# A hybrid decoder layer on one core: one softplus for both decays, bias tables read from memory, a minimum as the exponential's bias, and the planner's priorities set anew

## The chip, the cores and the metric

The program runs on one core of a Trainium2 chip. The metric is the time of one execution on the device in microseconds (us). The core has a matrix engine (TensorE, PE in the profile; PEld is its weight load), a vector engine (VectorE, DVE), a scalar engine (ScalarE, ACT), GpSimd (POOL) and a queue for DMAs (SyncE, SP). Each works through its own list of instructions in order and waits at semaphores for the others.

## The reference

One post-norm layer over 256 tokens of width 1024. A projection of the input gives the columns of four groups of six heads (head width 64); each group's output is multiplied by its own SiLU gate; the four are joined, projected back, added to the input and normalized.

```
proj = x @ w_in                              # 256 x 1024 by 1024 x 5906
a: softmax(q k / 8 - slope * dist) v         # causal; one block at this length
b: xbc = silu(conv4(xbc)); dt = softplus(dt_raw + dt_bias)
   y = ssd(xs * dt, -exp(A_log) * dt, B, C) + D * xs;  rms_norm(y * silu(z))
c: the three dilations of one head share a softmax: softmax(q k / 8 - slope * dist + ln count) v
d: q, k, v = silu(conv4(qkv)); q, k normalized; beta = sigmoid(b)
   g = -exp(A_log) * softplus(a + dt_bias);  gated delta rule in chunks, rms_norm, gate
out = layer_norm(2 ** 0.25 * x + concat(a, b, c, d) @ w_out)
```

In c a key that several dilations reach counts several times, so the mixture is one softmax whose scores carry the logarithm of the count.

## The kernel before

Weights arrive in blocks of up to 512 KB in a ring of four buffers (`raw`, line 403). Each block is split in two parts of lower precision: ACT copies the high part (`whi`), DVE subtracts it from the block (`wlo`), in `split` (line 418). PE multiplies high by high, high by low and low by high, three passes for each product, either with 128 weight columns as the stationary operand against all 256 tokens (`channels`, line 495) or with tokens as the stationary operand against 384 to 396 columns (`tokens`, line 517). These products, the stream, make up most of PE's work. The blocks come in the order: keys of d, gate d, queries of d (conv q), gate s, values c, values of d (conv v), conv bc, conv x, scores c, scores a, values a, and then the output weights.

Between these, small work is fed in. The delta path is: `softplus` of the decay (line 549), which is a chain of 16 DVE instructions and one ACT exponential on 12 numbers per partition; `decays` (line 566), which makes the decay matrix E; the products M and A (line 720); a triangular solve of 32 x 32 blocks on DVE, 31 steps over the tile Ub that read BL (line 785); a join on PE (line 798); and the delta rule itself (line 813). The state-space group has a softplus and a `decays` of its own (lines 750 to 755). Attention c and a (line 626) work on pairs of heads: PE makes scores, DVE adds the bias table, reduces to the row's maximum in the same instruction and writes p, a small DVE instruction multiplies the maximum by -0.125, ACT takes the exponential with that as its bias, divides, PE transposes and multiplies with the values. The bias table of c is computed by six DVE instructions (line 934), that of a by six ACT instructions (line 941) from constants `csb` that come in two loads early in the program (lines 448 and 450). The table of a (`biasa`) lies in the place s4, which BL has before it; that of c (`biasc`) lies in s3, which a block of the first weights has before it.

The order on each engine is not the program's. Every call is recorded with a modelled cost and its dependencies (`_Engine`, `Plan.add`), and `Plan.run` (line 200) then writes all orders out at build time. In each step it takes, over all engines, the instruction that can start first; among those of one engine that can start at about the same time (`AHEAD`) it takes the one with the longest way to the end plus the bias of its part in `PRIO`. Kinds of PSUM banks have limits (`LIMIT`) and are handed out in program order within a kind; a modelled cost is halved where two small matmuls lie side by side in the array. The engines then follow that order whatever the real times are.

Of the kernel before, what the change touches and what calls it, by code (L numbers as in the profile page):

```python
# [12 lines left out]
AF = mybir.ActivationFunctionType  # L13
# [13 lines left out]
LATE = ("moba", "dil", "lnc")  # L27


def _shape_constants():  # L30
    t = np.arange(128)
    row, col = t[:, None], t[None, :]
    parts = {
        "ident": row == col,
        "tri": row <= col,
        "suf": row > col,
    }
    dist = 128 + row - np.arange(256)[None, :]
    parts["moba"] = np.where(dist >= 0, -dist, -1e30)
    count = ((dist >= 0) & (dist <= 128)).astype(int) + ((dist >= 0) & (dist % 4 == 0)) \  # L40
        + ((dist >= 0) & (dist % 16 == 0))
    parts["dil"] = np.where(count > 0, -dist, -1e30)
    parts["lnc"] = 8.0 * np.log(np.maximum(count, 1))
    h = np.arange(6)[None, :]
    parts["sel"] = (row == h) | (row == 32 + h)
    at, n = {}, 0
    for k, v in sorted(parts.items(), key=lambda kv: kv[0] in LATE):
# [8 lines left out]
NEAR = CAT["moba"][0]  # L56
# [4 lines left out]
SWITCH, PORT, AHEAD = 0.17, 0.9, {"dve": 0.015, "pe": 0.185}  # L61
# [5 lines left out]
PRIO = {"split": -6.8, "conv k": 1086.3, "gate d": -51.1, "decay d": 1000.2, "norm k": 1627.6, "conv q": 1480.8,  # L67
        "products": 1504.1, "norm q": 1768.9, "gate s": 323.3, "decay s": -1394.4, "values c": 263.3,
        "conv v": 246.6, "blocks": 124.5, "join": -297.8, "delta": 975.5, "conv bc": -546.4, "conv x": -369.3,
        "state": 595.2, "scan": 1273.9, "scores c": -1234.3, "attention c": 2093.1, "scores a": -183.7,  # L70
        "values a": -1630.5, "attention a": -481.0, "out": 94.7, "out 0": -1157.7, "out 1": -1399.5,
        "ln 0": -2309.4, "ln 1": 877.3}
# [5 lines left out]
LIMIT = {"pj": 5, "g": 6, "ed": 1, "es": 5, "n": 6, "m": 4, "d": 4, "o": 1, "td": 5, "b": 2, "s": 2, "ts": 4, "c": 6, "ct": 5, "cv": 6, "a": 4, "at": 1, "av": 1}  # L78
BEGIN, SLOW = 1.2, 2.5


class Plan:
# [11 lines left out]
    def __init__(self, found=None):  # L94
        self.ops, self.tiles, self.tags, self.masks = [], {}, {}, {}
        self.after, self.bias, self.stream = None, 0.0, False
        self.found, self.made, self.slots = found, 0, {}

# [53 lines left out]
    def add(self, eng, call, cost, outs, ins, dma=0.0, mode=None, port=False, place=None, slow=0.0):  # L152
        i = len(self.ops)
        if self.found:
            self.ops.append({"id": i, "call": call, "dma": dma})
            return
        deps = {} if self.after is None else {self.after: 0.0}
        op = {"id": i, "bias": self.bias, "stream": self.stream, "eng": eng, "call": call, "cost": cost, "dma": dma,
              "mode": mode, "port": port, "place": place, "slow": slow, "deps": deps, "succ": [], "homes": []}
        self.ops.append(op)  # L160

        def dep(j, raw):
            if j != i:
                deps[j] = max(deps.get(j, 0.0), self.lat(j, eng) if raw or self.ops[j]["eng"] != eng else 0.0)

        for ap, write in [(a, False) for a in ins] + [(a, True) for a in outs]:
            info = self.tiles.get(ap.tensor.name)
            if info is None:
                continue
            p0, p1, m = self.region(info, ap)  # L170
            hit = lambda e: e[1] < p1 and p0 < e[2] and e[3] & m
            for e in info["w"]:
                if hit(e):
                    dep(e[0], True)
            if write:
# [24 lines left out]
    def run(self):  # L200
# [48 lines left out]
        while len(order) < len(ops):  # L249
# [22 lines left out]
            cost = o["cost"] * (0.5 if o["mode"] and o["mode"] == mode and o["place"] != place else 1.0)  # L272
# [94 lines left out]
def hybrid_layer(ctx, tc, plan, xT, x, w_in, w_out, convw, small, ln_g, ln_b, cst, out):  # L367
# [9 lines left out]
    def part(name):  # L377
        plan.bias = PRIO.get(name, 0.0)

# [60 lines left out]
    def constants():  # L440
# [54 lines left out]
    def channels(c0, n):  # L495

        for j in range(n // 128):
            hi, lo = split(load(w_in, 0, KC, c0 + j * 128, 128))
# [18 lines left out]
    def tokens(c0, n, raw=(), kinds=("pj", "pj")):  # L517

        bs = [bank(t) for t in kinds]
        for k0 in range(0, KC, 2):  # L520
            hi, lo = split(raw[k0 // 2] if k0 // 2 < len(raw) else load(w_in, k0 * 128, 2, c0, n))
# [6 lines left out]
        for i in range(2):  # L528
            yield i, bs[i]
# [90 lines left out]
    def scores(m, cols, tag):  # L620
        qk[m] = new(m + "qk", 2, 3, S, tag=tag)
        for n in range(2):
            for j, b in channels(cols[n], W):
                act.activation(qk[m][:, n, j, :], b, AF.Copy)

    def attention(m, k0, bias, tag):
# [5 lines left out]
        for pr in range(3):  # L632

            ss, pts = [bank(m) for _ in halves], []
# [4 lines left out]
            for e, s_ in enumerate(ss):  # L639
                h = 2 * pr + e  # L640
                p, mx = new("p", W), new("mx", 2, 2)
# [16 lines left out]
                pts.append(pt)  # L658
            b = bank(m + "v")
# [21 lines left out]
    beta, dav, gdec = new("beta", 2, 6), new("dav", 2, 6), new("gdec", 2, 6)  # L681
# [34 lines left out]
    part("conv q")  # L716
    for j, b in channels(D_Q, 256):
        conv(7 + j, b, kq[:, j, :, 1, :])
# [3 lines left out]
    for i in range(2):  # L722
        for pr in range(3):
            gb = [bank("m"), bank("m")]
# [93 lines left out]
    for i in range(2):  # L818
# [6 lines left out]
        for r in range(2):  # L825
            tp = slice(64 * r, 64 * r + 64)
# [11 lines left out]
        if i == 0:  # L838
# [5 lines left out]
            for e in range(2):  # L844
                q = slice(64 * e, 64 * e + 64)
                dve.tensor_copy(St[q, :, e, :], b[q, :3 * HD].rearrange("p (k d) -> p k d", k=3))
        ob = bank("o")
# [61 lines left out]
    for i in range(2):  # L909
        y = yd[:, i, :]  # L910
        b = bank("s")
# [22 lines left out]
    for h in range(NH):  # L934
        dve.scalar_tensor_tensor(bc[:, h, :], C("dil"), float(8 * SLOPES[h]), C("lnc"), op0=OP.mult, op1=OP.add)
# [5 lines left out]
    for h in range(NH):  # L941
        act.activation(ba[:, h, :], C("moba"), AF.Copy, scale=float(8 * SLOPES[6 + h]))
# [19 lines left out]
    for kk in order:  # L962
        part("out")
        plan.after = gate_in
# [100 lines left out]
```

## Time and profile before

| | us |
|---|---|
| median of 3 runs | 235.43 (235.09 to 236.21) |
| the profiled execution, whole | 235.13 |
| its span, first to last instruction | 233.4 |
| TensorE busy | 221.6 |
| VectorE busy | 178.6 |
| ScalarE busy | 142.2 |
| GpSimd busy | 22.3 |

The busy times are of the one profiled execution. A matmul's end is modelled in the profile and matmuls overlap, so the starts of successive matmuls tell PE's pace, and its busy time tells only where it had nothing at all. Nearly all instructions have the line of one helper (L356), so tiles and not lines tell the work apart: `ps` is any PSUM bank, `raw`, `whi`, `wlo` are the weight blocks, `sp` is the softplus's scratch, `mx` the row's maximum and sum, `p` the probabilities.

### The profile page before, as it was taken

The numbers are of one execution on the slowest core, as the hardware profiler recorded it, in microseconds if no ns is written. First come the engines' busy times: TensorE is split into PE (matmuls) and PEld (weight loads), VectorE is DVE, ScalarE is ACT, GpSimd is POOL, SyncE is SP. The second block draws the span as 40 slices with busy tenths as digits, with TensorE's granted clock in tenths as the row PEclk, the third lists the DMA queues.
The fourth block names the chain that finished last, engine by engine and source line by source line (L and its number), as shares of the span: only waits on it lengthen the run. The fifth ranks groups of instructions, "written<-read, shape, count | busy, mean of one in ns | idle before, by whom it ended". The sixth has DMA issues, their size and how long they took to land.

```text
span 233.4 us, 4547 instructions
## 1 busy us (share of the span) xinstructions
PE 221.6 (95%) x1679; PEld 198.2 (85%) x1679; DVE 178.6 (77%) x448; ACT 142.2 (61%) x300; POOL 22.3 (10%) x26
## 2 busy tenths in 40 slices
PE   7999999999999999899999999899999999999970
PEld 3999999699998999899888889697889988877870
DVE  2876999898869998899999996542579865464275
ACT  4777684656782544944669387999955547352210
POOL 3023020300020000000000000000023320000071
PEclk9999999999999999999999999999999999999997
DMA  6999627987550198666923524750525507550013
GB/s 177 357 368 325 186 84 200 272 215 212 144 152 14 18 262 237 172 183 179 260 79 81 145 73 128 192 161 4 176 94 183 179 4 246 204 180 3 0 67 113
DMA packets 45957, 36.92 MB, mean 158 GB/s; under 512 B 5600, under 2 KB 42592, under 8 KB 45936
## 3 DMA queue, kind: packets, MB, share of 16 engines
q1 hardware_dynamic: 45504, 36.25, 53.6%
q10 hardware_dynamic: 432, 0.39, 0.5%
q8 instruction: 13, 0.21, 0.3%
q14 instruction: 8, 0.07, 0.1%
HBM read 35.00 MB, written 1.64 MB: 157 GB/s over the span
## 4 chain that ended last, share of the span: by engine, by line
PE 42%; DVE 30%; DMA 11%; ACT 9%; issue 4%; SPq 2%; DVEq 0%; ACTq 0%
PE ps L356 42%; DVE wlo L356 10%; DMA raw<-in_w_in_dram 10%; DVE Ub L356 5%; DVE cy L356 4%; ACT whi L356 2%; DMA lead<-in_w_in_dram 2%; SPq L356 2%; DVE p L356 1%; DVE M L356 1%; DVE A L356 1%; ACT p L356 1%; ACT Ed L356 1%; DVE r L356 1%; ACT Tb L356 1%
## 5 line engine op out<-in xcount | busy, mean ns | idle before, releaser
L356 ACT ACTIVATE whi<-raw 128x1024 fp32r<-128x1024 f32 (+3 forms) x57 | 56.9, 1001 | 37.5 <-PE ps L356 25.6
L356 DVE TENSOR_TENSOR wlo<-raw,whi 128x1024 fp32r<-128x1024 f32 (+3 forms) x56 | 64.1, 1153 | 18.1 <-ACT whi L356 15.5
L356 PE MATMUL ps<-xhi,whi 128*128 128x256 f32 x272 | 42.0, 287 | 0.2 <-ACT whi L356 0.2
L356 PE MATMUL ps<-xhi,wlo 128*128 128x256 f32 x272 | 41.2, 285 | 0.0
L356 PE MATMUL ps<-xlo,whi 128*128 128x256 f32 x272 | 41.1, 285 | 0.0
L356 PEld LDWEIGHTS ps<-xhi,whi 128*128 128x128 f32 x272 | 35.8, 189 | 3.1 <-ACT whi L356 1.4
L356 PEld LDWEIGHTS ps<-xhi,wlo 128*128 128x128 f32 x272 | 35.7, 189 | 0.7 <-issue 0.7
L356 PEld LDWEIGHTS ps<-xlo,whi 128*128 128x128 f32 x272 | 35.7, 189 | 0.6 <-DVE xlo L356 0.2
L356 PE MATMUL ps<-whi,mix 128*128 128x512 f32 (+1 forms) x110 | 28.4, 349 | 0.0
L356 ACT ACTIVATE p<-p,mx 128x256 f32<-128x256 f32 (+1 forms) x48 | 19.6, 442 | 4.7 <-DVE mx L356 4.6
L356 PEld LDWEIGHTS ps<-whi,mix 128*128 128x128 f32 x110 | 19.2, 188 | 2.8
L356 DVE SCALAR_TENSOR_TENSOR cy<-ps,cw,cy 128x253 f32<-128x253 f32 (+2 forms) x48 | 19.9, 477 | 0.9 <-ACT cy L356 0.9
L356 PE MATMUL ps<-wlo,mix 128*128 128x512 f32 (+1 forms) x55 | 19.1, 353 | 0.0
L356 PE MATMUL ps<-whi,xlo 128*128 128x384 f32 (+2 forms) x64 | 17.6, 346 | 0.0
L356 PE MATMUL ps<-wlo,xhi 128*128 128x384 f32 (+2 forms) x64 | 17.1, 344 | 0.0
L356 PE MATMUL ps<-whi,xhi 128*128 128x384 f32 (+2 forms) x64 | 17.1, 345 | 0.0
L356 PEld LDWEIGHTS ps<-whi,xlo 128*128 128x128 f32 x64 | 11.5, 188 | 0.7 <-issue 0.7
L356 PEld LDWEIGHTS ps<-wlo,mix 128*128 128x128 f32 x55 | 10.3, 188 | 1.7 <-DVE wlo L356 0.4
L356 PEld LDWEIGHTS ps<-wlo,xhi 128*128 128x128 f32 x64 | 11.6, 188 | 0.0
L356 PEld LDWEIGHTS ps<-whi,xhi 128*128 128x128 f32 x64 | 11.3, 188 | 0.3 <-ACT whi L356 0.2
L356 POOL TENSOR_SCALAR_AFFINE_SELECT Es<-Es 128x1536 f32<-128x1536 f32 x1 | 1.5, 1548 | 101.2 <-ACT Es L356 101.2
L356 DVE TENSOR_TENSOR Ub<-BL,Ub 48x31 f32<-48x31 f32 (+15 forms) x31 | 10.3, 331 | 0.7
(226 smaller groups left out, 311.8 us busy)
## 6 DMA issues: line engine op xcount, KB each, us to landing
raw<-in_w_in_dram SPq DMA_DIRECT2D x30, 512.0 KB, 4.1
raw<-in_w_out_dram SPq DMA_DIRECT2D x12, 512.0 KB, 3.3
raw<-in_w_in_dram SPq DMA_DIRECT2D x8, 384.0 KB, 3.2
lead<-in_w_in_dram SPq DMA_DIRECT2D x7, 256.0 KB, 4.3
raw<-in_w_in_dram SPq DMA_DIRECT2D x4, 396.0 KB, 6.2
raw<-in_w_in_dram SPq DMA_DIRECT2D x4, 390.0 KB, 4.2
x<-in_x_dram SPq DMA_DIRECT2D x2, 512.0 KB, 3.7
xr<-in_xT_dram SPq DMA_DIRECT2D x7, 128.0 KB, 4.2
```

What stands on the lines that cost most here:

```text
L356: self.plan.add(eng, lambda: f(*a, **k), cost, outs, ins, dma, mode, port or (eng == "pool" and not dma), place, slow)
```

## The change

- One softplus serves both decays. The raw numbers of the state-space group and of the delta path are put side by side (12 + 12 per partition), and `softplus` runs once on 24. For this, conv q and gate s stand earlier in the program, and the new part "steps" follows gate s; both decays now depend on gate s and gate d.
- The bias tables of both attentions are made on the host, complete with slopes, logarithm of the counts and mask and with the opposite sign, and each is read by one DMA of 128 x 1536 numbers from SP's queue into the same places s3 and s4. The constants `moba`, `dil` and `lnc` are gone, and `csb` is one load.
- The queries are copied with the factor -0.125, so the scores in p have the opposite sign, the reduction takes the minimum, and the exponential uses the minimum as its bias with scale -1. The small multiplication of `mx` is gone.
- The planner gets other priorities for the parts, priorities for single steps of a part on single engines (`STEPS`, 28 entries), other limits on kinds of banks, an `AHEAD` for PE alone, and a modelled discount for neighbouring small matmuls that depends on their shape (`BESIDE`).

The number and the shapes of the matmuls are the same. The diff, cut to its core:

```diff
+def _biases():
+
+    dist = 128 + np.arange(128)[:, None] - np.arange(256)[None, :]
+    count = ((dist >= 0) & (dist <= 128)).astype(int) + ((dist >= 0) & (dist % 4 == 0)) \
+        + ((dist >= 0) & (dist % 16 == 0))
+    dil, moba = (np.where(m, -dist, -1e30).astype(np.float32)[:, None, :] for m in (count > 0, dist >= 0))
+    lnc = np.log(np.maximum(count, 1)).astype(np.float32)[:, None, :]
+    s1 = SLOPES[None, :, None]
+    return -np.concatenate([dil * s1[:, :6] + lnc, moba * s1[:, 6:]], 1).reshape(128, -1).astype(np.float32)
+
+
+BIAS = _biases()
...
-SWITCH, PORT, AHEAD = 0.17, 0.9, {"dve": 0.015, "pe": 0.185}
+SWITCH, PORT, AHEAD = 0.17, 0.9, {"pe": 0.172}
...
-PRIO = {"split": -6.8, "conv k": 1086.3, "gate d": -51.1, "decay d": 1000.2, "norm k": 1627.6, "conv q": 1480.8,
-        "products": 1504.1, "norm q": 1768.9, "gate s": 323.3, "decay s": -1394.4, "values c": 263.3,
...
+PRIO = {"split": -6.8, "conv k": 160.3, "gate d": -999.5, "conv q": 1973.4, "gate s": 577.1, "steps": 2980.3,
...
-LIMIT = {"pj": 5, "g": 6, "ed": 1, "es": 5, "n": 6, "m": 4, "d": 4, "o": 1, "td": 5, "b": 2, "s": 2, "ts": 4, "c": 6, "ct": 5, "cv": 6, "a": 4, "at": 1, "av": 1}
...
+STEPS = {"gate s 4": {"dve": -210.6}, "gate s 5": {"dve": -67.5}, "products 0": {"pe": -17.1},
...
+LIMIT = {"pj": 5, "g": 4, "ed": 6, "es": 4, "n": 5, "m": 5, "d": 6, "o": 2, "td": 5, "b": 1, "s": 2, "ts": 4, "c": 5, "ct": 4, "cv": 3, "a": 6, "at": 1, "av": 1}
 BEGIN, SLOW = 1.2, 2.5
+BESIDE = {(64, 128): 0.85, (128, 64): 0.62}
...
-        op = {"id": i, "bias": self.bias, "stream": self.stream, "eng": eng, "call": call, "cost": cost, "dma": dma,
+        op = {"id": i, "bias": self.bias + STEPS.get(self.step, {}).get(eng, 0.0), "stream": self.stream, "eng": eng, "call": call, "cost": cost, "dma": dma,
...
-            cost = o["cost"] * (0.5 if o["mode"] and o["mode"] == mode and o["place"] != place else 1.0)
+            cost = o["cost"] * (BESIDE[o["mode"]] if o["mode"] in BESIDE and o["mode"] == mode and o["place"] != place else 1.0)
...
         plan.bias = PRIO.get(name, 0.0)
+        plan.stage = plan.step = name
+
+    def step(n):
+        plan.step = "%s %d" % (plan.stage, n)
...
         sp.dma_start(sm, bass.AP(tensor=small.tensor, offset=small.offset, ap=[[0, 128], [1, NSM]]))
-        sp.dma_start(csb[:, :NEAR], cst[:, :NEAR])
-        plan.after = loads[CONST[2]]
-        sp.dma_start(csb[:, NEAR:], cst[:, NEAR:])
+        sp.dma_start(csb, cst)
         plan.after = None
...
-        t = new("sp", 6, 12)
-        ab, e, r, z, z2, p = (t[:, n, :].rearrange("p (a b) -> p a b", a=2) for n in range(6))
+        t = new("sp", 6, 24)
+        ab, e, r, z, z2, p = (t[:, n, :] for n in range(6))
...
+            plan.stage = "scores %s %s" % (m, "qk"[n])
             for j, b in channels(cols[n], W):
-                act.activation(qk[m][:, n, j, :], b, AF.Copy)
+                act.activation(qk[m][:, n, j, :], b, AF.Copy, scale=1.0 if n else -0.125)
...
-                                             scalar=-3e38, op0=OP.add, op1=OP.max, accum_out=mx[:, 0, n:n + 1])
-                dve.tensor_scalar(mx[:, 0], mx[:, 0], -0.125, None, op0=OP.mult)
+                                             scalar=3e38, op0=OP.add, op1=OP.min, accum_out=mx[:, 0, n:n + 1])
                 for c, n in parts:
-                    act.activation(p[:, c], p[:, c], AF.Exp, bias=mx[:, 0, n:n + 1], scale=0.125,
+                    act.activation(p[:, c], p[:, c], AF.Exp, bias=mx[:, 0, n:n + 1], scale=-1.0,
                                    accum_out=mx[:, 1, n:n + 1])
...
+    part("conv q")
+    for j, b in channels(D_Q, 256):
+        conv(7 + j, b, kq[:, j, :, 1, :])
+    part("gate s")
+    gz, raws = new("gz", 2, W), new("raws", 2, 6)
+    for i, b in tokens(S_Z, NZ):
+        gate(gz[:, i, :], b)
+        dve.tensor_copy(raws[:, i, :], b[:, W:NZ])
+    part("steps")
+    beta, v2, dt2, g2 = new("beta", 2, 6), new("v2", 2, 2, 6), new("dt2", 2, 2, 6), new("g2", 2, 2, 6)
     act.activation(beta, rawd[:, :, 0:6], AF.Tanh, scale=0.5)
     dve.tensor_scalar(beta, beta, 0.5, 0.5, op0=OP.mult, op1=OP.add)
-    dve.tensor_add(dav, rawd[:, :, 6:12], P("ddt")[:, None, :].to_broadcast([128, 2, 6]))
-    softplus(dav, gdec)
-    dve.scalar_tensor_tensor(gdec, gdec, -1.0, expA[:, 1:2, :].to_broadcast([128, 2, 6]), op0=OP.mult, op1=OP.mult)
+    for m, (r, n) in enumerate(((raws, "sdt"), (rawd[:, :, 6:12], "ddt"))):
+        dve.tensor_add(v2[:, m], r, P(n)[:, None, :].to_broadcast([128, 2, 6]))
+    softplus(v2.rearrange("p m a b -> p (m a b)"), dt2.rearrange("p m a b -> p (m a b)"))
+    for m in range(2):
+        dve.scalar_tensor_tensor(g2[:, m], dt2[:, m], -1.0, expA[:, m:m + 1, :].to_broadcast([128, 2, 6]), op0=OP.mult, op1=OP.mult)
+    dt, sda, gdec = dt2[:, 0], g2[:, 0], g2[:, 1]
...
-    part("conv q")
-    for j, b in channels(D_Q, 256):
-        conv(7 + j, b, kq[:, j, :, 1, :])
...
-    part("gate s")
-    gz, raws = new("gz", 2, W), new("raws", 2, 6)
-    for i, b in tokens(S_Z, NZ):
-        gate(gz[:, i, :], b)
-        dve.tensor_copy(raws[:, i, :], b[:, W:NZ])
-    sdv, dt, sda = new("sdv", 2, 6), new("dt", 2, 6), new("sda", 2, 6)
-    dve.tensor_add(sdv, raws, P("sdt")[:, None, :].to_broadcast([128, 2, 6]))
-    softplus(sdv, dt)
-    dve.scalar_tensor_tensor(sda, dt, -1.0, expA[:, 0:1, :].to_broadcast([128, 2, 6]), op0=OP.mult, op1=OP.mult)
...
     bc = new("biasc", NH, 256, tag="s3")
-    for h in range(NH):
-        dve.scalar_tensor_tensor(bc[:, h, :], C("dil"), float(8 * SLOPES[h]), C("lnc"), op0=OP.mult, op1=OP.add)
+    sp.dma_start(bc.rearrange("p h n -> p (h n)"), biases[:, 0:NH * 256])
...
     ba = new("biasa", NH, 256, tag="s4")
-    for h in range(NH):
-        act.activation(ba[:, h, :], C("moba"), AF.Copy, scale=float(8 * SLOPES[6 + h]))
+    sp.dma_start(ba.rearrange("p h n -> p (h n)"), biases[:, NH * 256:])
```

## Rows read from the trace of the kernel before

**Rows 1.** The page's busy line: engine, busy us, share of the span, instructions.
```profile
PE 221.6 (95%) x1679; PEld 198.2 (85%) x1679; DVE 178.6 (77%) x448; ACT 142.2 (61%) x300; POOL 22.3 (10%) x26
```

**Rows 2.** Busy time by stage: length, then each engine's us (instructions), clock, DMA.
```profile
4.84:45.40 40.56, 40.09 (x268) 37.97 (x268) 34.62 (x76) 29.08 (x56) 6.86 (x6) 1.00 0.83 255
...
84.00:100.00 16.00, 14.82 (x124) 14.35 (x123) 14.52 (x27) 10.46 (x17) 0.00 (x0) 1.00 0.79 213
100.00:145.00 45.00, 44.43 (x359) 40.72 (x358) 42.86 (x128) 28.76 (x70) 0.00 (x0) 1.00 0.52 139
145.00:157.00 12.00, 10.97 (x78) 9.50 (x78) 5.81 (x36) 11.91 (x42) 0.00 (x0) 1.00 0.74 197
...
185.00:226.40 41.40, 41.39 (x238) 33.92 (x236) 22.84 (x38) 16.87 (x26) 5.09 (x8) 1.00 0.31 108
226.40:233.40 7.00, 0.00 (x0) 0.00 (x0) 4.01 (x9) 0.00 (x0) 1.50 (x2) 0.76 0.32 112
```

**Rows 3.** Timeline of PE: start us, us, what, how many in one merged row.
```profile
100.80 1.11 PE L356 MATMUL ps<-xhi,wlo 128*128 128x256 f32 x8
101.75 1.11 PE L356 MATMUL ps<-xhi,whi 128*128 128x256 f32 x8
...
120.02 0.62 PE L356 MATMUL ps<-xhi,wlo 128*128 128x256 f32 x3
120.57 0.93 PE L356 MATMUL ps<-cqk 64*128 64x128 f32 x8
```

**Rows 4.** Groups by shape: busy us, mean ns, idle before, of the removed work.
```profile
L356 DVE SCALAR_TENSOR_TENSOR sp<-sp 128x12 f32<-128x12 f32 x16 | 2.7, 169 | 0.4
...
L356 DVE SCALAR_TENSOR_TENSOR biasc<-csb 128x256 f32<-128x256 f32 x6 | 2.4, 422 | 0.2 <-DMA csb<-in_cst_dram 0.2
...
L356 ACT ACTIVATE biasa<-csb 128x256 f32<-128x256 f32 x6 | 2.0, 401 | 0.0
...
L356 DVE TENSOR_SCALAR mx<-mx 128x2 f32<-128x2 f32 x12 | 1.9, 162 | 0.1
```

**Rows 5.** The chain that ended last, 145 to 152 us: start us, us, what.
```profile
145.82 1.53 ACT biasa L356 x5
...
149.92 1.76 ACT p L356 x7
```

**Rows 6.** Timeline of DVE, the delta path's softplus and what surrounds it.
```profile
39.72 0.17 DVE L356 SCALAR_TENSOR_TENSOR sp<-dav 128x12 f32<-128x12 f32 x1
...
43.80 0.17 DVE L356 COPY raws<-ps 128x6 f32<-128x6 f32 x1 [0.71 <-ACT workg L356]
...
55.91 0.17 DVE L356 SCALAR_TENSOR_TENSOR gdec<-gdec,expA 128x12 f32<-128x12 f32 x1
...
69.08 1.12 DVE L356 SCALAR_TENSOR_TENSOR M<-ps,rk,Ed 128x128 f32<-128x128 f32 x4
```

**Rows 7.** Timeline of SP's queue, early.
```profile
12.21 1.37 SPq L356 DMA_DIRECT2D csb<-in_cst_dram  x2
15.27 43.78 SPq L356 DMA_DIRECT2D raw<-in_w_in_dram  x19
```

**Rows 8.** Busy time of one early stretch, columns as in rows 2.
```profile
13.00:18.00 5.00, 5.00 (x41) 5.00 (x40) 2.88 (x4) 3.02 (x4) 1.89 (x2) 1.00 1.04 375
```

**Rows 9.** Timeline of ACT and weight loads; in brackets the idle time and what ended it.
```profile
22.46 1.06 ACT L356 ACTIVATE whi<-raw 128x1024 fp32r<-128x1024 f32 x1 [0.35 <-DMA raw<-in_w_in_dram]
...
23.57 1.01 PEld L356 LDWEIGHTS ps<-xhi,whi 128*128 128x128 f32 x8 [0.30 <-ACT whi L356]
```

**Rows 10.** Timeline of DVE, end of the solve and start of attention a.
```profile
142.81 0.18 DVE L356 TENSOR_TENSOR Ub<-BL,Ub 48x31 f32<-48x31 f32 x1
...
146.92 0.42 DVE L356 CUSTOM_DVE_ANT_0 p<-ps,biasa 128x256 f32<-128x256 f32 x1 [2.78 <-PE ps L356]
```

**Rows 11.** DMA issues of the page: KB each, median us to landing.
```profile
raw<-in_w_in_dram SPq DMA_DIRECT2D x30, 512.0 KB, 4.1
...
csb<-in_cst_dram SPq DMA_DIRECT2D x1, 384.0 KB, 7.3
```

More of the change, by code (lines that the diff above doesn't have):

```diff
@@ L26 @@
 SLOPES = (2.0 ** (-8.0 * (np.arange(12) + 1) / 12)).astype(np.float32)
-LATE = ("moba", "dil", "lnc")
 def _shape_constants():
@@ L37, in _shape_constants @@
     }
[L38 to L43, printed above, removed]
     h = np.arange(6)[None, :]
@@ L46, in _shape_constants @@
     at, n = {}, 0
-    for k, v in sorted(parts.items(), key=lambda kv: kv[0] in LATE):
+    for k, v in parts.items():
         at[k] = (n, v.shape[1])
@@ L55 @@
 NCST = CST.shape[1]
-NEAR = CAT["moba"][0]
+def _biases():
[7 more added lines that the diff above has]
+BIAS = _biases()
 SM = {"sdt": (0, 6), "ddt": (6, 6), "sA": (12, 6), "dA": (18, 6), "D": (24, 6), "dnw": (30, 64), "ssw": (94, 384)}
@@ L66 @@
 HOLD = {10: (("hold_hi", "cvg", 1), ("hold_lo", "s3", 1))}
-PRIO = {"split": -6.8, "conv k": 1086.3, "gate d": -51.1, "decay d": 1000.2, "norm k": 1627.6, "conv q": 1480.8,
-        "products": 1504.1, "norm q": 1768.9, "gate s": 323.3, "decay s": -1394.4, "values c": 263.3,
[L69 to L72, printed above, removed]
+PRIO = {"split": -6.8, "conv k": 160.3, "gate d": -999.5, "conv q": 1973.4, "gate s": 577.1, "steps": 2980.3,
+        "decay d": 2762.0, "norm k": 3290.6, "products": 310.1, "norm q": 4359.8, "decay s": -2381.1,
+        "values c": 537.5, "conv v": 131.6, "blocks": -433.8, "join": -2623.3, "delta": 2378.6, "conv bc": 108.8,
+        "conv x": -361.9, "state": -531.6, "scan": 1749.8, "scores c": -1768.9, "attention c": 7795.9,
+        "scores a": 6890.6, "values a": -6722.5, "attention a": 548.1, "out": -694.7, "out 0": -1620.4,
+        "out 1": -4315.5, "ln 0": -2452.3, "ln 1": -1777.2}
 CONST = -5, -4, -3
@@ L77 @@
 RINGS = {"raw": 4, "whi": 4, "wlo": 4}
-LIMIT = {"pj": 5, "g": 6, "ed": 1, "es": 5, "n": 6, "m": 4, "d": 4, "o": 1, "td": 5, "b": 2, "s": 2, "ts": 4, "c": 6, "ct": 5, "cv": 6, "a": 4, "at": 1, "av": 1}
+STEPS = {"gate s 4": {"dve": -210.6}, "gate s 5": {"dve": -67.5}, "products 0": {"pe": -17.1},
+         "products 2": {"pe": -177.9}, "values c 0": {"pe": 3.2}, "values c 1": {"pe": -245.8},
+         "conv v 0": {"dve": -218.5, "pe": -0.3}, "conv v 1": {"pe": 54.0}, "conv v 2": {"dve": -154.7},
+         "join": {"act": 251.9}, "conv bc 1": {"dve": 9.5}, "conv bc 2": {"dve": -24.3, "pe": -2.3},
[6 rows of a table added]
+LIMIT = {"pj": 5, "g": 4, "ed": 6, "es": 4, "n": 5, "m": 5, "d": 6, "o": 2, "td": 5, "b": 1, "s": 2, "ts": 4, "c": 5, "ct": 4, "cv": 3, "a": 6, "at": 1, "av": 1}
 BEGIN, SLOW = 1.2, 2.5
+BESIDE = {(64, 128): 0.85, (128, 64): 0.62}
 class Plan:
@@ L97, in __init__ @@
         self.found, self.made, self.slots = found, 0, {}
+        self.stage, self.step = "", ""
     def tile(self, pool, shape, dt, name, tag=None, bufs=1, kind=None):
@@ L366, in hybrid_layer @@
 @with_exitstack
-def hybrid_layer(ctx, tc, plan, xT, x, w_in, w_out, convw, small, ln_g, ln_b, cst, out):
+def hybrid_layer(ctx, tc, plan, xT, x, w_in, w_out, convw, small, ln_g, ln_b, cst, biases, out):
     nc = tc.nc
@@ L497, in channels @@
         for j in range(n // 128):
+            step(j + (c0 - S_B) // 128 if S_B < c0 < S_Z else j)
             hi, lo = split(load(w_in, 0, KC, c0 + j * 128, 128))
@@ L520, in tokens @@
         for k0 in range(0, KC, 2):
+            step(k0 // 2)
             hi, lo = split(raw[k0 // 2] if k0 // 2 < len(raw) else load(w_in, k0 * 128, 2, c0, n))
@@ L528, in tokens @@
         for i in range(2):
+            step(4 + i)
             yield i, bs[i]
@@ L632, in attention @@
         for pr in range(3):
+            step(4 * pr)
             ss, pts = [bank(m) for _ in halves], []
@@ L640, in attention @@
                 h = 2 * pr + e
+                step(4 * pr + e + 1)
                 p, mx = new("p", W), new("mx", 2, 2)
@@ L658, in attention @@
                 pts.append(pt)
+            step(4 * pr + 3)
             b = bank(m + "v")
@@ L680, in hybrid_layer @@
         dve.tensor_copy(rawd[:, i, :], b[:, W:ND])
-    beta, dav, gdec = new("beta", 2, 6), new("dav", 2, 6), new("gdec", 2, 6)
+    part("conv q")
[8 more added lines that the diff above has]
+    beta, v2, dt2, g2 = new("beta", 2, 6), new("v2", 2, 2, 6), new("dt2", 2, 2, 6), new("g2", 2, 2, 6)
     act.activation(beta, rawd[:, :, 0:6], AF.Tanh, scale=0.5)
     dve.tensor_scalar(beta, beta, 0.5, 0.5, op0=OP.mult, op1=OP.add)
-    dve.tensor_add(dav, rawd[:, :, 6:12], P("ddt")[:, None, :].to_broadcast([128, 2, 6]))
-    softplus(dav, gdec)
-    dve.scalar_tensor_tensor(gdec, gdec, -1.0, expA[:, 1:2, :].to_broadcast([128, 2, 6]), op0=OP.mult, op1=OP.mult)
+    for m, (r, n) in enumerate(((raws, "sdt"), (rawd[:, :, 6:12], "ddt"))):
[4 more added lines that the diff above has]
+    dt, sda, gdec = dt2[:, 0], g2[:, 0], g2[:, 1]
     part("decay d")
@@ L723, in hybrid_layer @@
         for pr in range(3):
+            step(3 * i + pr)
             gb = [bank("m"), bank("m")]
@@ L825, in hybrid_layer @@
         for r in range(2):
+            step(4 * i + r)
             tp = slice(64 * r, 64 * r + 64)
@@ L846, in hybrid_layer @@
                 dve.tensor_copy(St[q, :, e, :], b[q, :3 * HD].rearrange("p (k d) -> p k d", k=3))
+        step(4 * i + 2)
         ob = bank("o")
@@ L910, in hybrid_layer @@
         y = yd[:, i, :]
+        step(i)
         b = bank("s")
@@ L963, in hybrid_layer @@
         part("out")
+        step(kk)
         plan.after = gate_in
@@ L1045 @@
         "cst": CST,
+        "biases": BIAS,
     }
```

6 rows, old and new, of the table STEPS are left out of this document.

## The prediction

> **What bounds the kernel now.** I read the busy line first [rows 1]: TensorE (PE) 95%, VectorE (DVE) 77%, ScalarE (ACT) 61%. Then the same by stage [rows 2]. The reader is to see there that PE's idle time is small and sits in few places. Stage length less PE busy: 0.47 us up to 45.4 us, 1.18 us in 84 to 100, 0.57 us in 100 to 145, 1.03 us in 145 to 157, 0.01 us in 185 to 226.4. That is 3.3 us; after 226.4 us PE has nothing left, and the last layer norm and its store take 7.0 us more. In each of the two worst stages another engine is full: DVE 14.5 of 16.0 us in the first, ACT 11.9 of 12.0 us in the second. Third comes the timeline of PE [rows 3], because busy isn't pace. In a quiet stretch eight 128x256 matmuls start in 0.95 us (100.80 to 101.75), 0.118 us each. Amid attention three of the same take 0.55 us (120.02 to 120.57) where 0.35 is their pace: each return from small matmuls to the stream costs up to 0.2 us though PE is busy. So the bound is PE's own instruction stream, and the change leaves every matmul of it as it is; what can be had is idle time and those returns.
>
> **The change part by part.**
> One softplus for two: one call is 16 DVE instructions and one ACT exponential by the code, all on 128x12 tiles. The largest group takes 0.169 us each [rows 4], so about 16 x 0.17 = 2.7 us of DVE go. The remaining call works on 24 elements; 128x256 takes 0.422 us [rows 4], a slope of (0.422 - 0.169) / 244 = 1 ns an element, so 16 x 12 ns = 0.2 us come back.
> Bias tables loaded: six DVE instructions of 0.422 us (biasc, 2.4 us busy) and six on ACT (biasa, 2.0 us busy) go [rows 4].
> Minimum as the exponential's bias: the twelve small mx instructions go, 12 x 0.162 = 1.9 us of DVE [rows 4], each in the middle of a chain score, reduction, exponential. The factor -0.125 rides in a copy that ACT makes anyway: nothing.
> Together DVE loses 2.7 - 0.2 + 2.4 + 1.9 = 6.8 us of 178.6 and ACT 2.0 us of 142.2. None of that is PE time, so each piece counts only where PE waits:
> - 145 to 157 us: five of the six biasa instructions hold ACT from 145.82 on for 1.53 us, and the chain of waits then runs through ACT's p up to 151.7 us [rows 5], while PE idles 1.03 us. I take 0.9 us off.
> - 84 to 100 us: no removed instruction lies here; only the new order can help the 1.18 us. Nothing to all of it; I take half, 0.6 us.
> - Up to 45.4 us and 100 to 145 us: PE idles 0.47 + 0.57 us; six mx instructions (1.0 us of DVE) leave the second. I take 0.6 us of the 1.04.
> - Returns to the stream: each pair of heads has some four or five of them, six pairs in all; 6 x 4.5 x 0.15 = 4 us is the most that fewer or better-timed ones could bring, and minus as much if the order is worse. I take 0.9 us, near the small end, because the program still interleaves the same groups.
> The softplus of the delta path now waits for gate s too. Today it begins at 39.72 us, and its gdec ends only at 56.08 us; gate s gives its last raws at 43.97 us [rows 6]. The merged chain, about 17 steps of 0.2 us with the gap between them, could start at 44 and end near 47.4, so the added wait is covered by 8 us of slack. What is queued behind it on DVE are weight splits, whose readers on PE come later; if the order puts the chain last, the cover is the 13 us until M is made [rows 6]. Cost zero, bounds -0.3 to +1.
> The two loads are added on SP's queue. A table is 128 x 1536 x 4 bytes = 768 KB; 384 KB of constants go. The place of the first table's tile is free early, and SP issues nothing between the constants (12.21 + 1.37 us) and 15.27 us [rows 7], so I expect the table there, ahead of the weights of conv q. There the DMA engines are full at 375 GB/s [rows 8]: the net 384 KB are 1.05 us of queue, the whole table 2.1 us. Conv q's weights have no slack: ACT stands idle for their DMA until 22.46 us, and PE idles 0.30 us for that ACT copy at 23.57 us [rows 9]. So +1.05 us if the table is there, zero if it is put off; I take +0.4, since later the stream could wait on less than the full amount.
> The second table takes the place of BL, which the triangular solve reads until 142.99 us; the first use of the old one was at 146.92 us [rows 10]. A load of 512 KB lands in 4.1 us, one behind a full queue in 7.3 us [rows 11]. The 768 KB thus land between about 147 and 150 us: from nothing to +3 us on the start of that attention, with the weight stream of values a for PE to fill in. I take zero here, for a solve that also ends earlier on a freer DVE, and keep +2 as an end.
> Priorities, slots and the order on each engine are new altogether; no row of before shows that order. Its price is bounded by the same idle time and returns: -7.3 us to as much lost. It is inside the terms above.
> Sum: -0.9 - 0.6 - 0.6 - 0.9 + 0.4 = -2.6 us. The profiled execution took 235.13 us (span 233.4 and 1.7 around it): 232.5. The median of the runs shown is 235.43, 0.3 above it, so 232.8 us; its own range 230.5 to 234.2.
>
> **Rivals.**
> Nothing to measure (235.1): what goes is off PE and was hidden. For: PE 41.39 of 41.40 us busy in the out stage, 44.43 of 45.00 in the middle [rows 2]; the freed 6.8 us of DVE stand beside a full PE. Against: ACT at 11.9 of 12.0 with PE idle beside it.
> Slower (237.0): the first table ahead of conv q, at its full 1.05 to 2.1 us, since PE then has no other stream to run, with nothing regained; 235.4 + 1.6. It decides once the first split of conv q begins later than about 23.5 us. For: the gap on SP, full DMA engines [rows 8] and no slack [rows 9]. Against: the removed 384 KB pay half of it, and the planner that writes the order knows of the queue.
> Far faster (228.5): PE's 95% hides more room than its idle time. All 3.3 us of idle and most of the 4 us of returns go: 235.4 - 6.9. For: three matmuls at 0.55 instead of 0.35 us [rows 3]. Against: the out stage runs at pace with 41.39 of 41.40 us busy. The Trainium skill, page Perfetto Trace Analysis, section Identifying the Most-Contended Engine, says that matmul busy time is a bad measure of headroom and weight-load busy time a good one. By that rule the room would be the 15% in which no weights load [rows 1], some 35 us; in the out stage weight loads fill 33.92 of 41.40 us with PE at its pace for wider matmuls [rows 2], so the trace agrees with the first half of the rule and not with the second.
>
> **How the numbers follow.** Forecast 0.54, nothing 0.22, slower 0.17, far faster 0.07. One measurement of this kernel can tell about 0.5% (1.2 us) from no change, so faster is under 234.25 and slower over 236.6. Faster 0.54 + 0.07 = 0.61, same 0.22, slower 0.17. The range that holds 8 in 10 leaves out most of the far case and half of the slower one: 229.5 to 236.8 us; it holds the end with the early table (+1.05 with nothing regained) and the one with the second table late (+2 against -1.2).
>
> **What would show it.** DVE busy near 172 us, ACT near 140, PE's count 1679 and its stretch of full pace unchanged. No mx TENSOR_SCALAR, no biasc or biasa written by an engine, half of the sp instructions. PE idle under 0.3 us where attention a's exponentials start. The table's issue between 13 and 15 us, or not; the first split of conv q at or after 22.5 us. gdec before 56 us. Wrong would be: PE idle on a DMA of a bias table, PE's stages as long as before with the other engines idler (then all was hidden), or more than 4.6 us gained, which idle time plus the returns that I counted doesn't give.

## The result, and the profile after

The changed kernel takes 232.55 us (median of 4 runs, 231.78 to 233.27); the kernel before, on the same chip, 235.61 (4 runs). The ratio is 0.9869, interval 0.9826 to 0.9911: 1.3% faster. Forecast was 232.8. The profiled execution took 231.78 us, 3.35 less than the profiled one of before.

The page's busy line of the kernel after, answering to [rows 1]:

```profile
PE 217.0 (94%) x1679; PEld 198.1 (86%) x1679; DVE 175.3 (76%) x414; ACT 139.4 (61%) x293; POOL 20.6 (9%) x26
```

The work on DVE fell by 3.3 us with 34 instructions fewer, ACT by 2.8 us with 7 fewer. The matmuls are the same 1679, yet PE's busy time fell by 4.6 us. That is the first thing to see: no work left PE.

Busy time by stage of the kernel after (columns as in [rows 2]; the last two cuts are moved with the end of the matmuls):

```profile
4.84:45.40 40.56, 40.56 (x275) 40.04 (x276) 35.81 (x75) 28.70 (x55) 7.57 (x6) 1.00 0.84 267
45.40:84.00 38.60, 38.18 (x299) 35.76 (x297) 34.65 (x86) 24.50 (x45) 1.55 (x1) 1.00 0.68 174
84.00:100.00 16.00, 16.00 (x139) 16.00 (x138) 15.10 (x29) 10.38 (x19) 0.00 (x0) 1.00 0.72 185
100.00:145.00 45.00, 43.10 (x357) 39.72 (x355) 38.95 (x124) 30.23 (x78) 0.00 (x0) 1.00 0.60 166
145.00:157.00 12.00, 11.09 (x152) 9.89 (x153) 4.13 (x19) 11.95 (x39) 0.00 (x0) 1.00 0.44 116
157.00:185.00 28.00, 26.55 (x246) 23.98 (x244) 19.92 (x40) 16.59 (x35) 4.74 (x4) 1.00 0.30 95
185.00:223.00 38.00, 37.91 (x216) 31.65 (x214) 22.32 (x38) 14.95 (x22) 4.45 (x8) 1.00 0.34 118
223.00:230.10 7.10, 0.00 (x0) 0.00 (x0) 4.01 (x9) 0.00 (x0) 1.48 (x2) 0.86 0.31 111
```

Length less PE busy is now 0 up to 45.4 us (0.47 before), 0 in 84 to 100 (1.18), but 1.90 in 100 to 145 (0.57), 0.91 in 145 to 157 (1.03) and 1.45 in 157 to 185 (0.27). PE's idle time grew, and the kernel is faster all the same, because the time between one matmul's start and the next fell. The granted clock is 1.00 in every stage with matmuls, as before [rows 2], so it isn't the clock.

The timeline of PE after shows where the idle time went (in brackets: idle time before the row, and what ended it):

```profile
119.54 0.74 PE L374 MATMUL ps<-xhi,whi 128*128 128x256 f32 x4
121.06 0.55 PE L374 MATMUL ps<-csb,p 128*128 128x128 f32 x3 [0.79 <-ACT p L374]
...
143.55 0.34 PE L374 MATMUL ps<-wlo,xhi 128*128 128x384 f32 x1
145.62 0.55 PE L374 MATMUL ps<-csb,p 128*128 128x128 f32 x3 [1.73 <-ACT p L374]
```

Both are the first use of an attention's exponentials, at the start of attention c and of attention a. Ahead of the second one stands the second table. Timeline of DVE after, answering to [rows 10]:

```profile
136.76 0.18 DVE L374 TENSOR_TENSOR Ub<-BL,Ub 48x31 f32<-48x31 f32 x1
...
142.06 0.42 DVE L374 CUSTOM_DVE_ANT_0 p<-ps,biasa 128x256 f32<-128x256 f32 x1 [0.55 <-DMA biasa<-in_biases_dram]
```

and SP's queue after, both tables, answering to [rows 7]:

```profile
12.34 0.47 SPq L374 DMA_DIRECT2D biasc<-in_biases_dram  x1
12.85 0.53 SPq L374 DMA_DIRECT2D sm<-in_small_dram  x1
13.61 0.36 SPq L374 DMA_DIRECT2D csb<-in_cst_dram  x1
...
136.97 0.34 SPq L374 DMA_DIRECT2D biasa<-in_biases_dram  x1
```

The solve ends 6 us earlier (136.8 instead of 142.8), the table is issued right behind its last read and is the last thing DVE waits for, 0.55 us. The first table stands ahead of the constants, as feared. Yet PE, in the kernel after, comes to conv q without a gap:

```profile
24.51 0.52 PE L374 MATMUL ps<-whi,xhi 128*128 128x396 f32 x2
24.87 1.11 PE L374 MATMUL ps<-xhi,whi 128*128 128x256 f32 x8
```

ACT's first split of conv q in the same kernel:

```profile
23.27 1.05 ACT L374 ACTIVATE whi<-raw 128x1024 fp32r<-128x1024 f32 x1
```

It begins 0.8 us later than before (22.46 [rows 9]), but 44 of gate d's 48 matmuls (the ones with 396 columns) now stand ahead of conv q. In before it was 37, and PE turned to conv q at 23.58. The seven more, 0.18 us each, are the cover.

The softplus after, grouped by shape (ns: least, median, most):

```profile
L374 DVE SCALAR_TENSOR_TENSOR sp<-sp x8: 172/182/183, 47.8 to 51.1; 128x24 f32<-128x24 f32 x8
```

There is one call at 0.182 us an instruction where there were two at 0.169 [rows 4].

**Where the 3.4 us are.** From PE's timeline I took, for every matmul, the time from its start to the next one's start, less the idle time that the trace shows between them: its pace. "Stretches" counts how often PE comes to the weight stream from small matmuls. "First 40" is the part of the stream's pace that its first 40 matmuls took; they are the same, in the same order, in every kernel here. The small ones have in them 8 matmuls before the stream (3.6 us in before and after). All in us:

| profile of | stretches | stream's pace | of it the first 40 | small ones' pace | idle | sum |
|---|---|---|---|---|---|---|
| before | 60 | 174.4 | 5.3 | 46.9 | 3.7 | 225.1 |
| after | 46 | 172.0 | 5.5 | 44.7 | 4.9 | 221.6 |
| after, run again | 46 | 172.5 | 5.8 | 44.8 | 4.9 | 222.1 |
| after's order, work put back | 46 | 173.3 | 5.4 | 45.6 | 9.2 | 228.2 |
| before's order, work taken out | 60 | 174.8 | 6.0 | 46.7 | 5.6 | 227.1 |
| before, fewer returns | 46 | 172.7 | 5.7 | 49.2 | 6.7 | 228.6 |
| after, more returns | 60 | 175.5 | 7.0 | 45.3 | 4.4 | 225.2 |
| after, fewer returns | 32 | 170.0 | 5.6 | 47.0 | 6.4 | 223.4 |
| after with before's numbers | 62 | 175.7 | 6.3 | 48.2 | 6.6 | 230.4 |

After against before: stream -2.4, small ones -2.2, idle +1.2, together -3.4. The first 40 differ by up to 1.7 us between executions of the same instructions, so comparisons of the stream below leave them out; without them it is 169.1 us before and 166.5 after.

What a cheaper run of small matmuls looks like can be seen in eight `pt` (the products of the transposed probabilities with the values) of attention c in PE's timeline, before and then after:

```profile
127.74 1.27 PE L356 MATMUL ps<-pt,cvg 128*64 128x256 f32 x8
```

```profile
130.44 0.87 PE L374 MATMUL ps<-pt,cvg 128*64 128x256 f32 x8
```

In the shorter row they start two at a time, some 7 ns apart; in the longer one none start so close together. The experiments ask what made the pace, and what kept the idle time from eating it.

### The profile page after: what moved, and what is told of

It is laid out like the page before. It is cut to its first block, busy times and chain, and to the rows that moved or that the text cites. A ratio compares the mean times of both kernels' runs of the same rounds, so it can differ in the third digit from the quotient of the medians.

```text
span 230.1 us, 4524 instructions
## 1 busy us (share of the span) xinstructions
PE 217.0 (94%) x1679; PEld 198.1 (86%) x1679; DVE 175.3 (76%) x414; ACT 139.4 (61%) x293; POOL 20.6 (9%) x26
## 4 chain that ended last, share of the span: by engine, by line
PE 58%; DVE 22%; ACT 9%; DMA 5%; issue 4%; DVEq 0%; SPq 0%; ACTq 0%
PE ps L374 58%; DVE wlo L374 8%; ACT p L374 3%; ACT whi L374 2%; DMA raw<-in_w_in_dram 2%; DVE cy L374 2%; DMA U<-dU 2%; DVE yd L374 2%; ACT Es L374 1%; DMA xr<-in_xT_dram 1%; DVE mix L374 1%; DVE r L374 1%; DVE Es L374 1%; DVE Ub L374 1%; DVE gd L374 1%
## 5 line engine op out<-in xcount | busy, mean ns | idle before, releaser
L374 DVE TENSOR_TENSOR wlo<-raw,whi 128x1024 fp32r<-128x1024 f32 (+3 forms) x56 | 64.8, 1166 | 23.3 <-ACT whi L374 21.7
L374 PE MATMUL ps<-xlo,whi 128*128 128x256 f32 x272 | 43.4, 286 | 0.0
L374 PE MATMUL ps<-xhi,wlo 128*128 128x256 f32 x272 | 40.7, 283 | 0.0
L374 PEld LDWEIGHTS ps<-xhi,whi 128*128 128x128 f32 x272 | 36.5, 190 | 2.6 <-ACT whi L374 1.3
L374 PEld LDWEIGHTS ps<-xlo,whi 128*128 128x128 f32 x272 | 37.4, 190 | 0.5 <-issue 0.3
L374 PE MATMUL ps<-whi,mix 128*128 128x512 f32 (+1 forms) x110 | 29.0, 351 | 0.0
L374 DVE SCALAR_TENSOR_TENSOR cy<-ps,cw,cy 128x253 f32<-128x253 f32 (+2 forms) x48 | 21.0, 474 | 0.9 <-ACT cy L374 0.7
L374 ACT ACTIVATE cy<-ps,cw 128x256 f32<-128x256 f32 x16 | 8.7, 555 | 4.7 <-DVE cw L374 2.0
L374 DVE TENSOR_TENSOR Ub<-Ub 48x31 f32<-48x31 f32 (+15 forms) x31 | 10.3, 333 | 0.7
```

The costliest lines, as they stand in the source:

```text
L374: self.plan.add(eng, lambda: f(*a, **k), cost, outs, ins, dma, mode, port or (eng == "pool" and not dma), place, slow)
```

## Experiments

Theory O: the gain is the new order of the matmuls. Theory W: it is the work taken from DVE and ACT. "Aligned" below means that the start of each matmul is compared with that of the same matmul in another run of the same order. Ratios are to the kernel before in the same series.

**The change once more, in two series.** No edit.

> The changed kernel once more, beside the kernels that it is compared with here. Both theories: ratio to before 0.983 to 0.991, some 232.5 us, 46 stretches of the weight stream on TensorE against 60 before.

> The changed kernel once more, beside the three that follow: ratio to before 0.982 to 0.989.

232.34 us, ratio 0.9847 (0.9808 to 0.9886), and 232.27, 0.9845 (0.9809 to 0.988). The gain holds, and this is the base of the rest.

**After's order with the old work put back.** Every engine keeps its order; behind the planned instructions stand 34 on DVE and 7 on ACT more, of the shapes that the change removed:

```diff
+ also(lambda k=k: V.scalar_tensor_tensor(p2, p2, 1.0 / k, y2, op0=OP.add, op1=OP.mult))     # a second softplus, 128x12
+ also(lambda mx=mx: nc.vector.tensor_scalar(mx[:, 0, 0:1], mx[:, 0, 0:1], 1.0, None, op0=OP.mult))    # 12 of these
+ also(lambda: nc.vector.scalar_tensor_tensor(tb, csb[:, 0:256], 0.5, csb[:, 128:384], ...))     # 6, in the first conv parts
+ also(lambda: [nc.scalar.activation(tba, csb[:, 0:256], AF.Copy, scale=0.5) for _ in range(6)]) # behind Tb
```

> The changed kernel with its order on every engine, and the removed work put back right behind instructions of that order: 12 small multiplications of mx in their chains, a second softplus of 16 DVE and 1 ACT instructions on 12 numbers, six DVE instructions of 128x256, six ACT instructions of 128x256 behind Tb (34 DVE, 7 ACT; 6.8 and 2.4 us). Theory O (the gain is the new order: fewer returns to the stream and no idle PE before 120 us) expects at most 1.0 us more than the changed kernel, most of it where ACT copies delay attention a. Theory W (the gain is the work taken off DVE and ACT) expects 2.5 us or more, back to the time of before.

238.49 us, ratio 1.0101 (1.0058 to 1.0143): slower even than before. W looks confirmed, but see what the lag is made of. Aligned with the first of the two repeats above, it is a staircase that hardly comes down: +0.7 at 29.5 us, +0.6 at 36, +0.7 at 41 (the six table instructions), nothing between 50 and 57 us (the whole second softplus), +0.7 at 129 to 133 (mx), +2.2 from 141.5 to 146 (the six copies on ACT) and +0.3 at 150; 0.6 stood already at 9.5 us, before any edit. The timeline of ACT in this kernel, and then PE's:

```profile
141.34 2.12 ACT L374 ACTIVATE Tb<-Ub 48x1024 f32<-48x1024 f32 x1
143.37 2.65 ACT L844 ACTIVATE tba<-csb 128x256 f32<-128x256 f32 x6
145.92 0.37 ACT L374 ACTIVATE aqk<-ps 128x256 f32<-128x256 f32 x1
```

```profile
144.27 0.92 PE L374 MATMUL ps<-aqk 64*128 64x128 f32 x6
146.34 2.01 PE L374 MATMUL ps<-aqk 64*128 64x128 f32 x18 [1.16 <-ACT aqk L374]
...
151.79 0.44 PE L374 MATMUL ps<-csb,p 128*128 128x128 f32 x2 [1.83 <-ACT p L374]
```

The copy of attention a's queries waits behind the six, and PE behind it. So where an instruction stands decides its price here: the 17 of the softplus cost nothing, six copies 2 us. Where I put the DVE tables isn't where before had them, so their 1.9 us are not the price of before's.

**Before's order with the work out.** The tables are loaded, mx and the state-space softplus go, nothing else moves:

```diff
                 dve.tensor_scalar(mx[:, 0], mx[:, 0], -0.125, None, op0=OP.mult)
+                instead()     # planned, but not written into the program
...
-    softplus(sdv, dt)
+    softplus(sdv, dt, True)     # two of its 17 instructions are left
...
+        instead(lambda h=h: nc.sync.dma_start(bc.rearrange("p h n -> p (h n)"), biases[:, 0:NH * 256]) if h == 0 else None)
                              # the table's load in place of the six, as early as its place allows
```

> The kernel before with its order on every engine, and the removed work taken out: no multiplication of mx, bias tables by two DMAs (the first where the far constants were loaded, the second once BL is free), and of the state-space group's softplus 14 DVE instructions and the exponential left out (its step sizes are then not the reference's). 32 DVE and 7 ACT instructions fewer, 6.8 and 2.2 us. Theory O expects a gain of 0 to 1.0 us, with 60 stretches as before. Theory W expects 2.5 us or more. The prediction's rival of the early table expects PE to wait about 1 us longer near 23.6 us.

237.42 us, ratio 1.0058 (1.0027 to 1.009): slower, which neither theory had, with DVE 4.4 us less busy. W falls as the whole cause. PE's timeline in this kernel:

```profile
23.79 0.34 PE L373 MATMUL ps<-whi,xhi 128*128 128x396 f32 x1
25.19 1.21 PE L373 MATMUL ps<-xhi,whi 128*128 128x256 f32 x8 [1.05 <-ACT whi L373]
```

and its ACT:

```profile
21.03 0.21 ACT L373 ACTIVATE expA<-sm 128x12 f32<-128x12 f32 x1 [1.76 <-DMA sm<-in_small_dram]
...
22.74 1.45 ACT L373 ACTIVATE cy<-ps,cw 128x256 f32<-128x256 f32 x3
24.09 2.95 ACT L373 ACTIVATE whi<-raw 128x1024 fp32r<-128x1024 f32 x3
```

The same `expA` on ACT in the kernel before:

```profile
19.14 0.20 ACT L356 ACTIVATE expA<-sm 128x12 f32<-128x12 f32 x1
```

This is the forecast's slower rival in its size: the early table ahead of conv q, the split at 24.09 instead of 22.46 us [rows 9], PE idle 1.05 us. The path is another. The split doesn't wait for conv q's weights here; ACT stands idle 1.76 us for `sm`, a small load that is now queued behind the table, and then its list has the copies of constants and three `cy` ahead of the split. The rest of the aligned lag against before is mainly 0.5 at the start, +0.6 at 97.5 (bcT), -0.6 at 117 and 126 (where mx is gone), +0.5 from 148 to 152 (the second table late, the ACT copies gone). The pace is before's, 221.5 against 221.3 us.

**Returns to the stream alone.** A rule on PE's order, all else equal: in before and in after, 14 short stretches of the stream are moved ahead of the small matmuls in front of them; in after, also the reverse, two stream matmuls into the middle of 14 runs of small ones.

```diff
+        order = self.merge(order, 8, 14)      # before: 60 to 46 stretches; after: 46 to 32
...
+        order = self.part_up(order, 14)       # after: 46 to 60
```

> The kernel before, nothing of its work changed; in the order of PE alone 14 short stretches of the weight stream (8 matmuls or fewer) go ahead of the small matmuls that stood before them, so that 46 stretches are left of 60, as many as the changed kernel has. Theory O expects 14 x 0.1 to 0.2 us, a gain of 1.4 to 2.8 us, less what the moved matmuls wait for their weights. Theory W expects no gain beyond 0.3 us.

> The changed kernel, nothing of its work changed; in the order of PE alone two stream matmuls go into the middle of a run of small ones, 14 times, so that there are 60 stretches again. Theory O expects 1.4 to 2.8 us more than the changed kernel. If the number of returns doesn't matter and only idle time does: within 0.4 us of it.

> The changed kernel with 14 short stretches of the stream moved ahead of the small matmuls before them: 32 stretches instead of 46. Theory O expects 1.4 to 2.8 us less, unless the small matmuls that come later delay the ACT work that waits for them. If returns don't matter: no gain, or a loss from later small matmuls.

Before with fewer: 238.58, ratio 1.0103 (1.0069 to 1.0137), slower. After with more: 234.26, 0.9921 (0.9891 to 0.9951), as O expected; its profiled execution, at 235.3, was above that median. After with fewer: 233.91, 0.99 (0.9874 to 0.9926). Both moves away from after's 46 lose (0.992 and 0.99 against 0.985). In the table the stream behaves as the forecast said. Without the first 40, a return costs it (169.1 - 167.0) / 14 = 0.15, (168.5 - 166.7) / 14 = 0.13 and (166.7 - 164.3) / 14 = 0.17 us. But where stretches of the stream were moved away, the small matmuls slow down by 2.2 to 2.3 us and PE idles 1.5 to 2.9 us more. So fewer returns alone are no gain; after's own order has them together with cheaper small ones (44.7 against 46.9). O in the short form "fewer returns" falls too.

**The numbers of the planner alone.** The program after, planned with before's priorities, limits, `AHEAD` and discount and no `STEPS`; and the program before with after's priorities, limits and `AHEAD`.

```diff
-PRIO = {... "steps": 2980.3, ...}     # after's
+PRIO = {... "gate s": 323.3, ...}     # before's
-STEPS = {"gate s 4": ...}
+STEPS = {}
```

> The changed program with the planner's numbers of before (PRIO with the new part steps at gate d's value, LIMIT, AHEAD, no STEPS, the flat half for neighbouring small matmuls); the planner writes the order anew. If the removed work alone brought the gain: ratio under 0.995. If the order must be made for the program (the first eight runs speak for that): above 1.00, 236 us or more, some 60 stretches.

> The program before with the changed PRIO, LIMIT and AHEAD (STEPS has no counterpart there); the planner writes the order anew. If the new priorities alone brought the gain: ratio under 0.995. If the order must be made for the program: above 1.00, 236 us or more, though it has fewer stretches than before.

240.53 us, ratio 1.0185 (1.0134 to 1.0235), and 243.23, 1.0288 (1.0255 to 1.0321). Numbers made for one program are worse on the other, both ways. The first of the two has PE's pace at 223.9 us, 7 above after's (6 without the first 40), at the same work: the order alone makes that much. Which of the priorities, `STEPS`, the limits and the discount makes it wasn't separated.

The second time isn't only the order's. Its mean granted clock over whole executions was 0.968 to 0.975, and 0.929 in the profiled one (253.16 us); in before's it is 0.989 to 0.996. From the profiled execution, a row of PE's timeline and one of busy time (columns as in [rows 2]):

```profile
166.59 0.91 PE L356 MATMUL ps<-vb,U 64*64 64x64 f32 x12 [3.20 <-ACT U L356]
```

```profile
167.90:198.40 30.50, 29.93 (x166) 28.07 (x167) 15.92 (x31) 8.59 (x19) 4.33 (x3) 0.50 0.22 70
```

PE stood idle for 3.20 us, and the granted clock then was at its lower level (1.2 GHz) up to 198.4 us. By 157 us PE had started nearly as many matmuls as before had (1105 against 1119). How much of the 243.23 us the order would cost at the full clock isn't shown.

**The tables' places.** The first table loaded late, behind BL; the second early, at the same point, in a place of its own; and the second in its own place in a lull of the queue, behind the ninth weight load after BL:

```diff
-    ba = new("biasa", NH, 256, tag="s4")
+    ba = new("biasa", NH, 256, tag="ba" if plan.found else "s4")
...
+            order.insert(order.index(self.mark[j]) + 1, w)      # w: the table's load, j: BL
```

> The changed kernel, same order but for one DMA: the bias table of attention c is loaded right behind BL instead of at 12.3 us. If the early table delays conv q's weights into PE: the first split of conv q begins about 1 to 2 us earlier and 0.4 to 1 us are gained. If the rest of gate d that stands before conv q covers it: the split begins earlier, PE's time does not change beyond 0.2 us.

> The changed kernel, same order but for one DMA: the bias table of attention a has a place of its own and is loaded right behind BL, some 40 us earlier. If the late table holds PE at the start of attention a: 0.5 to 0.6 us less (DVE's 0.55 us of idle time for that DMA goes, and PE's 1.7 us behind ACT's p shrink by as much). If ACT's own work in that stage sets it: no change beyond 0.2 us.

> The changed kernel, same order but for one DMA: the table of attention a has a place of its own and is loaded in the lull of the DMA engines, behind the weight load that is issued at 117.8 us, instead of at 137 us. From the run that loaded it behind BL: the 0.43 us that PE gained at the start of attention a stay, the 0.99 us that it lost at attention c's scores go: 0.3 to 0.6 us less than the changed kernel, 0.998 of it. If the loss at 119 us was not the DMA's: a loss again.

Table c late: 234.47, ratio 0.9927 (0.9899 to 0.9955). Aligned, nothing is won before 90 us against the first profile of after, and 0.3 us against the first repeat, so in after's order the early table costs next to nothing. At its new place it delays a weight split (DVE idles 2.11 us for ACT's `whi` at 110.19), and attention c pays 1.6 us against that repeat. PE's timeline in this kernel, and its busy time a little later:

```profile
120.09 0.92 PE L378 MATMUL ps<-cqk 64*128 64x128 f32 x4 [1.44 <-DVE mx L378]
```

```profile
121.30:124.50 3.20, 2.70 (x14) 2.41 (x13) 2.63 (x11) 2.67 (x10) 0.00 (x0) 0.50 0.35 104
```

Behind that wait the granted clock stood at 0.50, the lower level (1.2 GHz), from 121.2 to 124.6 us, and the lag grew from 0.8 to 1.8 us there: 1.0 us more, which is the clock's and not the table's directly. The mean granted clock was 0.978 to 0.988 in eleven of this kernel's twelve executions; in the kernel after it was 0.989 to 0.996 in fourteen of sixteen.

Table a early: 233.7, 0.9898 (0.9862 to 0.9935). BL now lands in 5.9 us instead of 4.6 to 4.7 and the solve starts at 102.9 instead of 100.8 to 101.5, which costs PE 1.0 us at attention c. The same alignment shows 0.43 us won at attention a. The median hides two groups: four executions at a mean clock of 0.989 to 0.992 took 232.65 to 233.15 us, 0.984 of before's median and so no more than the kernel after; the other four, at 0.981 to 0.985, took 234.24 to 235.84. The profiled one is of the first four, so the loss in the median goes with the clock, and no trace shows where it fell. Table a in the lull: 231.66, 0.9816 (0.9785 to 0.9847), with the unchanged kernel at 232.27 in the same series. Its PE timeline at attention a:

```profile
145.93 0.55 PE L379 MATMUL ps<-csb,p 128*128 128x128 f32 x3 [1.11 <-ACT p L379]
```

1.11 us idle instead of 1.73 (1.56 in the first repeat): the late table costs 0.5 to 0.6 us here. In this profile a weight load that landed 1 us late (ACT idle to 108.65, ahead of the table's issue at 119.15) took as much away at attention c, so the profiled time shows no gain. It is the fastest kernel measured, by 0.6 us, but the intervals overlap: the gain is likely, not shown.

## Why the prediction was right, and where it wasn't

The time and the sign came out: -2.6 forecast, -3.35 between the two profiles, -3.06 between the medians. The sum is right through errors that cancel, so its closeness is luck; what held is that PE's own list bounds the kernel, that no removed work counts by itself, and the price of a return.

- **145 to 157 us, -0.9: failed.** ACT's copies are gone, but ACT is as full as before (11.95 of 12.0) since the stage now holds more of attention a, and the wait for p moved to 145.62 and grew to 1.73 us. The sign that I set, PE idle under 0.3 us there, didn't come. Idle time in 100 to 157 us went from 1.60 to 2.81.
- **84 to 100 us, -0.6, and up to 45.4 us and 100 to 145, -0.6: mixed.** The first lost all its 1.18 us, the early one its 0.47; the middle one grew by 1.33 instead. All idle terms together were forecast at -2.1; the trace has +1.2, and where I had nothing it grew, from 0.27 to 1.45 in 157 to 185 us and from 0.02 to 0.42 in 45.4 to 84.
- **Returns, -0.9: mis-sized, and the name too narrow.** The pace of PE fell by 4.6 us. The 14 returns account for 1.8 to 2.4 us of stream (0.13 to 0.17 each; the forecast had 0.15), within my bound of 4. That bound counted 27 returns of the two attentions; before has 60 stretches in all, so the price was right and the number too small. The 2.2 us of the small matmuls were in no term: the 24 `kq,kT` went from 4.5 to 3.9 us, the 48 `pt` of both attentions from 6.3 to 5.3, with `cqk` 0.4 dearer. Matmuls that start within 30 ns behind another small one rose from 11 to 18 among the `pt` and from 4 to 10 among the `kq,kT`, and fell from 12 to 6 among the `cqk`, each time the way the price went. That is read from the traces; no run changes these neighbours alone, so the cause of that half isn't tested.
- **Early table, +0.4: next to nothing here, and 1.05 us in before's order.** The price was real, by another path than the forecast's: ACT waited for `sm` behind the table, not for conv q's weights. So the match with the forecast's 1.05 us of queue doesn't confirm its path. The new order takes more of gate d ahead and gives cover. The condition for it (a first split later than 23.5 us) fits both: 23.27 in after, 24.09 where it cost. The 0.30 us of [rows 9] are idle time of the weight loads; PE's own row at 23.58 shows none.
- **Merged softplus, 0: nearly right.** It ran from 46.0 to 51.5 us, later and longer than forecast (44 to 47.4), with the decays done by 51.7; before's gdec ended at 56.08 [rows 6]. PE waits 0.20 us for DVE's `cumd` behind it at 53.33, inside the bounds.
- **Second table, 0: +0.4 to +0.6**, inside the bounds. The solve did end earlier, as the forecast hoped, by 6 us.
- **DVE "near 172 us": 175.3.** 34 instructions went as counted. The durations of all DVE records, added up, fell by 7.4 us (205.1 to 197.7), near the 6.8 forecast; the busy time, in which overlapping records count once, only by 3.3. Here the sum of durations was no forecast of busy time.

What neither the forecast nor its rivals said: the parts don't add. The work out of the old order costs 0.6%, the new order with the old work 1.0%, together they gain 1.3 to 1.5%. The order gives PE its pace (219 to 217 us against 221 to 224). With the work put back that order idles 9.2 us instead of 4.9, so it seems to run close behind DVE and ACT and to need the room that the removed work leaves; as I chose where to put the work back, this is argued and not shown.

The Trainium skill, page Perfetto Trace Analysis, section Identifying the Most-Contended Engine, calls matmul busy time a bad measure of headroom. By the trace this is so in a sense I hadn't used: PE's busy time fell by 4.6 us with the same matmuls, so it held time that shows as work and isn't needed. The far-faster rival was built on just this and was cut down to 0.07. The pace it named for returns (most of 4 us) did come in size, though only about half of it from returns, and idle time took a quarter of it back.

## What to carry to other kernels

On an engine that is 95% busy, count the time from start to start, by kind and by neighbour, before counting idle time: the larger part of this gain was in it. An order worked out for one set of instructions is part of that set: here a test of either alone gave the wrong sign. A small edit to a tuned order is best priced at each place where something is queued behind it, and the path named by the row that waits. A load added in the middle of the stream was paid here by what stood next to it in the queue, so try it where the queue is quiet, in a place that is free early. Before a longer time is put down to an edit, read the granted clock of each execution.

## What the runs showed that I had not expected

- A lag was hardly ever made up. In the kernel with the work put back, some ten steps of 0.3 to 1.3 us add up to 6.1 us at the last matmul; no more than 0.2 us came back at any one place on the way.
- Executions differ before any edit: at 9.5 us, where PE has run the same matmuls in all kernels here, they stand 0.1 to 0.8 us from another execution of the same order, one of them 1.8 us. Where no edit lies before 90 us, 0.2 to 0.7 us of lag is there at that point. So up to 0.8% of a single comparison of profiles can be the start.
- A load of 768 KB far from its use cost 1.0 and 1.6 us of PE, by way of BL or of a weight load landing later, with DVE 38.95 of 45 us busy behind them in the kernel after. The clock added 1.0 us to the second.
